# The convolution branch's layer norm between the first units of the seven-product gate, and down sums issued closer together, in a two-layer encoder trunk on one Trainium2 core

## The chip, the core and the metric

The kernel runs on one core of one Trainium2 chip. PE multiplies matrices, DVE and ACT do elementwise work on tiles of 128 partitions, POOL does a little of that and issues DMAs, SP only issues DMAs. Each engine executes its own list of instructions in order and waits for others by semaphores. The metric is device time in microseconds (us), smaller is better; the median of several runs is compared.

## What is computed

Two layers of an encoder over 512 tokens of width 1024, float32. In each, one projection of the normalized input feeds four branches (a convolution branch, neighbourhood, dilated and windowed attention), each of width 256. Every branch is projected to 1024 channels, multiplied by its own sigmoid gate, and the four are summed, projected and added to the input. A ConvFFN follows. Cut to what bears on this change:

```python
def _conformer_conv(a_in, conv_w, conv_b, ln_g, ln_b):
    a, g = jnp.split(a_in, 2, axis=-1)
    u = a * jax.nn.sigmoid(g)
    u = _depthwise_conv(u, conv_w, conv_b)          # width 31
    u = _layernorm(u, ln_g, ln_b)                   # over the 256 channels
    return jax.nn.silu(u)

ys = jnp.stack([y_a, y_b, y_c, y_d], axis=2)
branch = jnp.einsum('bsnc,ncd->bsnd', ys, w_branch[l])
gates = jax.nn.sigmoid(gate_pre.reshape(bsz, seq, N_BRANCH, D_MODEL) + gate_b[l])
mixed = jnp.sum(gates * branch, axis=2)
x = x + mixed @ w_out[l]
x = x + _conv_ffn(_rmsnorm(x, g_ffn[l]), w_up[l], ffn_conv_w[l], ffn_conv_b[l], w_down[l])
```

## The kernel before

**Products and weights.** Activations lie with channels on partitions and the 512 tokens along the free dimension. A float32 product is made of three: the high part of the weights times the high and the low part of the activations, and the low part of the weights times the high part (`prod`, lines 290 to 292). Weights come in units of 128x1024: one load on SP's queue into `w_raw` (two buffers), one ACT instruction for the high half `w_hi` (line 269), one DVE instruction for the low half `w_lo` (line 271), three buffers each. `unit()` asks for a unit one ahead of the one used. A block of 128 output channels is 24 matmuls of 128x128 by 128x512 into one bank. There are eight PSUM banks, four with the tag `mm` and four with `aux`.

**Order.** The program traces the work in one sequence, and a planner turns it into a list for each engine, by priority and by its own estimate of when each instruction is ready. Weight units are put 3000 places ahead. Side work is written as generators. After each half block and each block the main line calls `tick()`: every generator in `side` then runs on to its next `yield`, and what it issues on PE comes after the last matmul so far. `tick()` also adds `self.pace` to a credit (`served`); while that isn't below zero, the next of the down sums is issued and its price, 9, is taken off. `finish(g)` ticks until one generator is done.

**Down sums.** `weight_sums` makes sums of the down projection's weights for a scheme with seven products in place of eight. A layer has 24 transfers between places in DRAM, of 0.75 or 1 MB, copying or accumulating (line 1283). They go on POOL's queue, and each waits for the last matmul at the place where it was traced (`paced`). The credit begins at -40 with a pace of 4.0 where the values are projected; the pace is 2.7 from the end of the windowed attention's projection on.

**The stretch around the change.** In `layer`, after the four branches' projections, `gates(n)` runs for the neighbourhood, dilated and windowed branch (`ORDER[0]`, `[1]`, `[2]`). A gate has eight blocks d. Each block multiplies by the norm (line 860), takes a tanh (line 862) and ticks twice; from d = 2 on, `branch(n, d - 2)` multiplies the branch's output with its own weights (6 matmuls). For the second and third gate line 1005 makes a product of it and the gate on DVE, and line 1006 adds it to `mixed` on POOL. Beside these gates run the attentions and `conv`, the convolution's 60 taps on DVE (line 457), each traced behind a matmul.

When the first half of the third gate and the windowed attention are done, the attention's pool is closed, a pool `outp` is opened, and `gate_forms` is put into `side`: for four pairs of channel blocks, POOL loads the layer's input (line 885, two loads of 256 KB each, paced), ACT multiplies by the gain (line 896), DVE forms four differences and sums (lines 901 to 904), and ACT and DVE split the result (lines 906 and 907). Then the second half of the third gate is traced. `conv`, when its taps are done, goes on to the layer norm as it comes: 8 transposes on PE into two `aux` banks (line 470), statistics on DVE (lines 473 and 474), a Newton iteration for the inverse root (lines 477 and 324 to 329), normalization into `cv` tiles (line 486), 8 transposes back into two `aux` banks (line 495), scale and shift on ACT (line 499), a tanh (line 501) and products and a split (lines 502 to 504) into `Y[0]`. `while self.side: self.tick()` drains all this before the last gate.

**The seven-product gate.** `last_gate` is the convolution branch's gate. `GATE_STEPS` lists 14 units of 24 matmuls of 128x128 by 128x256 (line 935), seven for each half of the channels (`ga`, `gb`): A11 and A12 take the plain input, the others but S4 a form. Each unit ticks twice. Unit A12 uses an `mm` bank for a moment, the others keep four `aux` banks. The raw weights grow in place: after the low half of a unit is made (line 1275), POOL adds the next quarter by an accumulating DMA (line 1256). `gate_done` writes tanh tiles `ths`; after the units 12 and 14 come four branch products each, with `Y[0]`.

Of the kernel before, what the change touches and what calls it, by code (L numbers as in the profile page):

```python
# [14 lines left out]
F32 = mybir.dt.float32  # L15
# [3 lines left out]
ALU = mybir.AluOpType  # L19
# [3 lines left out]
P = 128  # L23
L = 2
D = 1024
S = 512
# [66 lines left out]
ORDER = (1, 2, 3, 0)  # L93
# [137 lines left out]
class Trunk:  # L231
# [214 lines left out]
    def conv(self):  # L446

        nc = self.nc
        v = nc.vector
        accs = []  # L450
        for j in range(2):
            u = self.glu_u[j]
            acc = self.gp.tile([P, 542], F32, name="cv", tag="cv", bufs=4)[:, :S]
            w = lambda t: self.par('a_conv_w', j * 31 + t)
            v.tensor_scalar(acc, u[:, 0:S], w(0), self.par('a_conv_b', j), ALU.mult, ALU.add)
            for t in range(1, 31):
                self.after_mm(v.scalar_tensor_tensor(acc, u[:, t:t + S], w(t), acc, ALU.mult, ALU.add))  # L457
                if t % 5 != 2:
                    yield
            accs.append(acc)  # L460
        yield
        mv = self.norm.tile([P, NB, 2], F32, name="mv", tag="mv", bufs=1)
        st = self.norm.tile([P, NB, 6], F32, name="bst", tag="bst", bufs=1)
        pss = []
        for h in range(2):
            ps = self.aux()
            for b in range(2):
                for j in range(2):
                    tb = 2 * h + b
                    nc.tensor.transpose(out=ps[:, (b * 2 + j) * P:(b * 2 + j + 1) * P],  # L470
                                        in_=accs[j][:, tb * P:(tb + 1) * P], identity=self.ident)
            for b in range(2):
                v.bn_stats(st[:, 2 * h + b, :], ps[:, b * 256:(b + 1) * 256])
                v.bn_aggr(mv[:, 2 * h + b, :], st[:, 2 * h + b, :])
            pss.append(ps)
        ve = self.norm.tile([P, NB], F32, name="ms", tag="ms", bufs=2)
        v.tensor_scalar(ve, mv[:, :, 1], 1.0, EPS, ALU.mult, ALU.add)
        r = self.norm.tile([P, NB], F32, name="rln", tag="rln", bufs=1)
        self.rsqrt(self.norm, ve, [P, NB], r)
        yield  # L480
        uns = []
        for h in range(2):
            un = self.gp.tile([P, 542], F32, name="cv", tag="cv", bufs=4)
            for b in range(2):
                tb = 2 * h + b
                v.tensor_scalar(un[:, b * 256:(b + 1) * 256], pss[h][:, b * 256:(b + 1) * 256], mv[:, tb, 0:1],
                                r[:, tb:tb + 1], ALU.subtract, ALU.mult)
            uns.append(un)
        for _ in range(2):
            yield  # L490
        yh, yl = self.y_tiles()
        for j in range(2):
            ps = self.aux()
            for tb in range(NB):
                nc.tensor.transpose(out=ps[:, tb * P:(tb + 1) * P],
                                    in_=uns[tb // 2][:, (tb % 2) * 256 + j * P:(tb % 2) * 256 + (j + 1) * P],
                                    identity=self.ident)
            z = self.gp.tile([P, 542], F32, name="cv", tag="cv", bufs=4)
            nc.scalar.activation(z[:, :S], ps, AF.Identity, scale=self.par('ln_g', j), bias=self.par('ln_b', j))
            th = self.gp.tile([P, S], F32, name="th", tag="th", bufs=3)  # L500
            nc.scalar.activation(th, z[:, :S], AF.Tanh, scale=0.5)
            v.scalar_tensor_tensor(z[:, :S], th, 1.0, z[:, :S], ALU.add, ALU.mult)
            nc.scalar.activation(yh[:, j, :], z[:, :S], AF.Copy, scale=0.5)
            v.scalar_tensor_tensor(yl[:, j, :], z[:, :S], 0.5, yh[:, j, :].bitcast(F32), ALU.mult, ALU.subtract)
            yield
        self.Y[0] = (yh, yl)
# [433 lines left out]
    def gate_done(self, g, n, ps):  # L940

        nc = self.nc
        v = nc.vector
        if n in ('A11', 'S3', 'S2'):
            tag, bufs = ("th", 3) if n == 'S2' else ("t1", 2) if n == 'A11' else ("xn", 2)
            t = self.svs[g, n] = (self.op if n == 'S3' else self.gp).tile([P, S], F32, name="sv", tag=tag, bufs=bufs)
            with self.first():
                nc.scalar.activation(t, ps, AF.Copy)
        if n == 'S2':
            r, h = 1, 0  # L950
            v.tensor_tensor(t, self.banks[g, 'B'], t, ALU.subtract)
        elif n == 'A12':
            r, h, t = 0, 0, self.svs[g, 'A11']
            v.tensor_tensor(t, t, ps, ALU.add)
        elif n == 'S1':
            r, h, t = 1, 1, self.svs[g, 'S3']
            with self.first():
                v.tensor_tensor(t, t, ps, ALU.subtract)
        elif n == 'S4':
            r, h, t = 0, 1, self.gp.tile([P, S], F32, name="sv", tag="th", bufs=3)  # L960
        else:
            return
        two = lambda t: t.rearrange("p (e q) -> p e q", e=2)
        cols = slice(h * 256, (h + 1) * 256)
        half = self.RB[:, cols].unsqueeze(1).broadcast_to([P, 2, 256])
        v.tensor_tensor(two(t), two(ps if n == 'S4' else t), half, ALU.mult)
        for e in range(2):
            d = 4 * 'ab'.index(g[1]) + 2 * (1 - r) + e
            if h == 0:
                pool, tag, bufs = (self.gp, "cv", 4) if r == 0 else (self.op, "xr", 2) if g == 'ga' else (self.op, "sq", 2)  # L970
                self.ths[d] = pool.tile([P, 542 if r == 0 else S], F32, name="th", tag=tag, bufs=bufs)[:, :S]
            c = ORDER[3] * 8 + d
            nc.scalar.activation(self.ths[d][:, cols], t[:, e * 256:(e + 1) * 256], AF.Tanh, scale=0.5,
                                 bias=self.gbh[:, c:c + 1])
# [12 lines left out]
    def branch(self, n, d, bu, th, q=None):  # L987
        nc = self.nc
        v = nc.vector
        while self.Y[n] is None:  # L990
            self.tick()
        yh, yl = self.Y[n]
        q = d % 4 if q is None else q
        ps = self.mm()
        for k in range(2):
            s = slice((q * 2 + k) * P, (q * 2 + k + 1) * P)
            self.prod(ps, bu[0][:, s], bu[1][:, s], yh[:, k, :], yl[:, k, :], k == 0, k == 1)
        if n == ORDER[0]:
            m = self.gp.tile([P, S], F32, name="mx", tag="mx", bufs=8)
            self.mixed.append(m)  # L1000
            v.scalar_tensor_tensor(m, th, 1.0, ps, ALU.add, ALU.mult)
            return
        m = self.mixed[d]
        t = self.gp.tile([P, S], F32, name="t1", tag="t1", bufs=2)
        v.scalar_tensor_tensor(t, th, 1.0, ps, ALU.add, ALU.mult)
        (v if n == ORDER[3] else nc.gpsimd).tensor_tensor(m, m, t, ALU.add)
        if n == ORDER[3]:
            if d % 2 == 0:
                self.mixed_parts = [self.op.tile([P, 1024], F32R, name=x, tag=f"{x}{d // 2}", bufs=1) for x in ("mh", "ml")]
            mh, ml = (x[:, d % 2 * S:(d % 2 + 1) * S] for x in self.mixed_parts)  # L1010
            nc.scalar.activation(mh, m, AF.Copy, scale=0.5)
            v.scalar_tensor_tensor(ml, m, 0.5, mh.bitcast(F32), ALU.mult, ALU.subtract)
            self.MH[d] = mh, ml
# [550 lines left out]
    def layer(self, l):  # L1564
# [3 lines left out]
        with tc.tile_pool(name="gate", bufs=1, reuse_waits="tile") as self.gp:  # L1568
            with tc.tile_pool(name="attn", bufs=1, reuse_waits="tile") as self.ap:
# [18 lines left out]
                ready = self.beside(self.qk_stats(Q, 4, 4, 0))  # L1588
                self.queue(chain(ready, self.qk_norm(Q, 4, 4, 2), self.attention('dil', Vd, 2)))
                self.glu()  # L1590
                self.side.append(self.conv())
                V = self.new_V()
                Q = self.project_swa(V)
                ready = self.beside(self.qk_stats(Q, 4, 2, 2))
                swa = chain(ready, self.qk_norm(Q, 4, 2, 4), self.attention('swa', V, 3))
                self.queue(swa)
                self.pace = 2.7
                for n in ORDER[:2]:
                    self.gates(n)
                self.gates(ORDER[2], range(4))  # L1600
                self.finish(swa)
            with tc.tile_pool(name="outp", bufs=1, reuse_waits="tile") as self.op:
                self.gate_forms()
                self.gates(ORDER[2], range(4, 8))
                while self.side:
                    self.tick()
                self.last_gate()
                self.pace = 0.0
                self.xnew = self.new_res()
# [82 lines left out]
```

## Time and profile before

| | us |
|---|---|
| median of 3 runs (lowest, highest) | 1567.18 (1567.09, 1567.3) |
| the profiled execution | 1566.39 |
| its span, first to last instruction | 1564.6 |
| PE busy within the span | 1535.1 |
| DVE busy | 1309.2 |
| ACT busy | 942.6 |
| POOL busy | 201.1 |

The mean granted TensorE clock of this execution is 0.992. A line of the time line gives the start in us, the time from the first start to the last end in us, the engine, the line of the kernel, the operation, output and inputs with their shapes, the count and, in brackets, how long the engine stood idle before it and what ended that. Durations of neighbouring matmuls overlap, so the distance of starts says how fast PE goes on.

### The profile page before, as it was taken

How to read it: one execution, taken by the hardware profiler on the slowest of the kernel's cores; microseconds unless marked ns; L12 is line 12 of the kernel's file. 1: busy time of each engine (PE TensorE's matmuls, PEld its weight loads, DVE VectorE, ACT ScalarE, POOL GpSimd, SP SyncE). 2: the span in 40 equal slices, each digit the busy share in tenths (PEclk: the TensorE clock that was granted, in tenths of full speed). 3: DMA queues.
4: the chain of work that ended last, by engine and by line, in shares of the span. 5: the costliest groups of instructions: out<-in, count | busy, mean ns of one | idle time of the engine just before them, and what ended most of it. 6: DMA issues, size and time to landing. Idle time of an engine off the chain costs nothing.

```text
span 1564.6 us, 22903 instructions
## 1 busy us (share of the span) xinstructions
PE 1535.1 (98%) x8274; PEld 1326.2 (85%) x8274; DVE 1309.2 (84%) x2202; ACT 942.6 (60%) x1580; POOL 201.1 (13%) x296
## 2 busy tenths in 40 slices
PE   9999999979999999999999999999799999999999
PEld 8888888859888999888888888888698899998887
DVE  6689988777879998997576899887777899999974
ACT  5678777345456665564457687673454556655643
POOL 0123002322001110000001130023310011100000
PEclk9999999989999999999999999999899999999999
DMA  7788565766565886256558796657666589962564
GB/s 233 226 227 192 158 148 146 188 150 149 185 205 117 183 185 162 97 196 205 183 177 257 202 200 158 141 149 191 151 154 204 187 168 225 196 162 95 185 225 162
DMA packets 117153, 278.58 MB, mean 178 GB/s; under 512 B 27440, under 2 KB 29360, under 8 KB 117040
## 3 DMA queue, kind: packets, MB, share of 16 engines
q1 hardware_dynamic: 87088, 187.98, 37.1%
q0 software_dynamic: 29664, 88.62, 29.1%
q8 instruction: 65, 1.06, 0.3%
q10 hardware_dynamic: 288, 0.52, 0.1%
q14 instruction: 48, 0.39, 0.1%
HBM read 259.25 MB, written 58.72 MB: 203 GB/s over the span
## 4 chain that ended last, share of the span: by engine, by line
PE 87%; DVE 6%; DMA 3%; ACT 3%; issue 1%; POOL 0%; DVEq 0%; ACTq 0%; POOLq 0%
PE mm L291 14%; PE mm L292 14%; PE mm L290 14%; PE aux L1127 9%; PE aux L935 4%; PE aux L1375 3%; PE aux L1374 3%; PE aux L1373 3%; PE mm L519 2%; PE mm L521 2%; PE mm L520 2%; PE mm L1375 2%; PE mm L1374 2%; PE mm L1373 2%; PE aux L812 2%; PE aux L789 2%
## 5 line engine op out<-in xcount | busy, mean ns | idle before, releaser
L269 ACT ACTIVATE w_hi<-w_raw 128x1024 fp32r<-128x1024 f32 (+1 forms) x241 | 251.3, 1043 | 236.0 <-PE mm L291 82.3
L271 DVE TENSOR_TENSOR w_lo<-w_raw,w_hi 128x1024 fp32r<-128x1024 f32 (+1 forms) x241 | 290.9, 1208 | 69.1 <-ACT w_hi L269 67.6
L290 PE MATMUL mm<-xh,w_hi 128*128 128x512 f32 x768 | 300.9, 392 | 0.0
L291 PE MATMUL mm<-xl,w_hi 128*128 128x512 f32 x768 | 300.3, 391 | 0.0
L292 PE MATMUL mm<-xh,w_lo 128*128 128x512 f32 x768 | 299.8, 390 | 0.0
L292 PEld LDWEIGHTS mm<-xh,w_lo 128*128 128x128 f32 x768 | 144.5, 188 | 30.6
L290 PEld LDWEIGHTS mm<-xh,w_hi 128*128 128x128 f32 x768 | 144.7, 188 | 29.1
L291 PEld LDWEIGHTS mm<-xl,w_hi 128*128 128x128 f32 x768 | 144.6, 188 | 28.4
L1127 PE MATMUL aux<-form,w_hi 128*128 128x256 f32 x768 | 140.3, 284 | 0.7 <-ACT sv L1139 0.7
L1127 PEld LDWEIGHTS aux<-form,w_hi 128*128 128x128 f32 x768 | 120.0, 192 | 1.8 <-ACT sv L1139 1.5
L1127 PE MATMUL aux<-form,w_lo 128*128 128x256 f32 x384 | 108.7, 283 | 0.0
L1274 ACT ACTIVATE w_hi<-chain 128x1024 fp32r<-128x1024 f32 x64 | 67.6, 1057 | 57.5 <-DMA chain<-W 15.1
L1275 DVE TENSOR_TENSOR w_lo<-chain,w_hi 128x1024 fp32r<-128x1024 f32 x64 | 77.9, 1219 | 23.1 <-ACT w_hi L1274 23.1
L457 DVE SCALAR_TENSOR_TENSOR cv<-cv,prm 128x512 f32<-128x512 f32 x120 | 94.0, 783 | 0.7
L1168 ACT ACTIVATE cy<-U,prm 128x512 f32<-128x512 f32 x88 | 68.4, 808 | 32.6 <-DVE U L1213 21.0
L519 PE MATMUL mm<-w_hi,xh 128*128 128x512 f32 x192 | 76.4, 398 | 0.4 <-DVE V L647 0.4
L520 PE MATMUL mm<-w_lo,xh 128*128 128x512 f32 x192 | 75.0, 391 | 0.0
L521 PE MATMUL mm<-w_hi,xl 128*128 128x512 f32 x192 | 74.8, 390 | 0.0
L1127 PEld LDWEIGHTS aux<-form,w_lo 128*128 128x128 f32 x384 | 73.7, 192 | 0.0
L1256 POOL DMA_DIRECT2D chain<-W x48 | 42.1, 878 | 240.3 <-DVE w_lo L1275 240.3
L1274 ACT ACTIVATE w_hi<-w_raw 128x1024 fp32r<-128x1024 f32 x48 | 50.6, 1053 | 36.2 <-PE aux L1127 19.8
L776 ACT ACTIVATE e<-e,rl 128x256 f32<-128x256 f32 (+2 forms) x96 | 57.3, 597 | 21.8 <-DVE rl L775 21.4
(376 smaller groups left out, 3865.5 us busy)
## 6 DMA issues: line engine op xcount, KB each, us to landing
w_raw<-W SPq DMA_DIRECT2D x191, 512.0 KB, 4.1
sums<-W POOLq DMA_DIRECT2D x24, 1024.0 KB, 11.5
chain<-W POOLq DMA_DIRECT2D x48, 512.0 KB, 5.4
w_raw<-W SPq DMA_DIRECT2D x66, 256.0 KB, 3.8
w_raw<-sums SPq DMA_DIRECT2D x44, 256.0 KB, 3.6
w_raw<-sums SPq DMA_DIRECT2D x22, 512.0 KB, 4.2
sums<-W POOLq DMA_DIRECT2D x12, 768.0 KB, 8.8
sums<-sums POOLq DMA_DIRECT2D x8, 1024.0 KB, 7.0
```

Of the source, the lines that this page charges most:

```text
L269: w = nc.scalar.activation(hi[:, s], raw[:, s], AF.Copy)
L271: nc.vector.tensor_tensor(lo[:, s], raw[:, s], hi[:, s].bitcast(F32), ALU.subtract)
L290: mm(ps, lhsT=wh, rhs=xh, start=start, stop=False)
L291: mm(ps, lhsT=wh, rhs=xl, start=False, stop=False)
L292: self.last_mm = mm(ps, lhsT=wl, rhs=xh, start=False, stop=stop)
L457: self.after_mm(v.scalar_tensor_tensor(acc, u[:, t:t + S], w(t), acc, ALU.mult, ALU.add))
L519: mm(pss[b], lhsT=self.Xh[k][:, t], rhs=hi[:, s], start=k == 0, stop=False)
L520: mm(pss[b], lhsT=self.Xh[k][:, t], rhs=lo[:, s], start=False, stop=False)
L521: self.last_mm = mm(pss[b], lhsT=self.Xl[k][:, t], rhs=hi[:, s], start=False, stop=k == KT - 1)
L1127: self.last_mm = nc.tensor.matmul(o, lhsT=w[:, s], rhs=x, start=start and not (e or j or i), stop=j == 3 and i == 2, skip_group_check=True)
L1274: nc.scalar.activation(hi, raw, AF.Copy)
L1373: mm(ps, lhsT=x[0], rhs=w[0][:, cols], start=start, stop=False, skip_group_check=again)
```

## The change

It touches the order of the work and some buffers, and no product.

- `conv` waits after its taps until `self.closing` is set, and then makes the layer norm. `closing` is set after the third gate when the forms are done, just ahead of `last_gate`, so that the layer norm's steps are traced at the ticks of the first units of that gate. Only the forms are waited for ahead of it, not all side work.
- The layer norm's four banks are `mm` banks in place of `aux` banks.
- The last gate's tanh tiles of the half with r = 0 lie in `yh` and `yl` buffers in place of `cv` buffers.
- In the third gate, the adds of line 1006 with d of 4 and more, four a layer, go from POOL to DVE.
- The pace of the down sums is 3.6 in place of 2.7 from the first gate on.

```diff
@@ conv
-        yield
+        while not self.closing:
+            yield
...
-            ps = self.aux()
+            ps = self.mm()
...
         yh, yl = self.y_tiles()
         for j in range(2):
-            ps = self.aux()
+            ps = self.mm()
@@ gate_done
-            if h == 0:
-                pool, tag, bufs = (self.gp, "cv", 4) if r == 0 else (self.op, "xr", 2) if g == 'ga' else (self.op, "sq", 2)
-                self.ths[d] = pool.tile([P, 542 if r == 0 else S], F32, name="th", tag=tag, bufs=bufs)[:, :S]
+            if h == 0 and r == 1:
+                self.ths[d] = self.op.tile([P, S], F32, name="th", tag="xr" if g == 'ga' else "sq", bufs=2)
+            elif h == 0 and e == 0:
+                x = self.gp.tile([P, 2, S], F32, name="th", tag="yh" if g == 'ga' else "yl", bufs=2)
+                self.ths[d:d + 2] = x[:, 0], x[:, 1]
@@ branch
-        (v if n == ORDER[3] else nc.gpsimd).tensor_tensor(m, m, t, ALU.add)
+        (v if n == ORDER[3] or n == ORDER[2] and d >= 4 else nc.gpsimd).tensor_tensor(m, m, t, ALU.add)
@@ layer
                 self.glu()
+                self.closing = False
                 self.side.append(self.conv())
...
-                self.pace = 2.7
+                self.pace = 3.6
...
                 self.gate_forms()
+                forms = self.side[-1]
                 self.gates(ORDER[2], range(4, 8))
-                while self.side:
-                    self.tick()
+                self.finish(forms)
+                self.closing = True
                 self.last_gate()
```

## The prediction

> **What bounds the kernel now.** I read the page first, then the waits of PE, then PE's time line where it stops, and last the time lines of ACT, DVE and POOL at those places.
>
> ```profile
> span 1564.6 us, 22903 instructions
> ...
> PE 1535.1 (98%) x8274; PEld 1326.2 (85%) x8274; DVE 1309.2 (84%) x2202; ACT 942.6 (60%) x1580; POOL 201.1 (13%) x296
> ```
>
> PE is busy for 98% of the span, so an edit can only pay where PE stops or where its clock is low. Its idle time is 1564.6 - 1535.1 = 29.5 us. The waits of PE say where (waiter, what ended the wait: us in total, times, longest):
>
> ```profile
> PE aux L495 <- DVE cv L486: 13.0, 2, 6.6
> PE mm L290 <- ACT w_hi L269: 6.4, 2, 4.2
> PE aux L935 <- DVE w_lo L1275: 3.1, 4, 0.9
> ```
>
> Two waits, each once in each layer, make 19.4 us of the 29.5. Both sit at the end of the third gate; line 495 is the second transposition of the layer norm, which the change moves. Here is PE in layer 0:
>
> ```profile
> 328.42 0.80 PE L290 MATMUL mm<-yh,w_hi 128*128 128x512 f32 x1 [4.24 <-ACT w_hi L269]
> 335.64 0.69 PE L495 MATMUL aux<-cst,cv 128*128 128x128 f32 x2 [6.42 <-DVE cv L486]
> ...
> 338.68 0.63 PE L292 MATMUL mm<-yh,w_lo 128*128 128x512 f32 x1
> ...
> 340.39 0.63 PE L290 MATMUL mm<-xh,w_hi 128*128 128x512 f32 x1
> ...
> 345.08 0.39 PE L292 MATMUL mm<-xh,w_lo 128*128 128x512 f32 x1
> ...
> 349.84 0.39 PE L292 MATMUL mm<-yh,w_lo 128*128 128x512 f32 x1
> ```
>
> The reader is to see three losses: PE waits 4.24 us for the high half of a weight unit, then 6.42 us for the normalized tile, and then its clock is halved: from 338.68 to 340.39 matmuls start 0.43 us apart (four steps), from 345.08 to 349.84 they start 0.227 us apart (21 steps). The stretches from the end of the last matmul before the first wait to the first matmul of the seven-product gate give the sum (length; busy time and count of PE, PEld, DVE, ACT, POOL; granted clock, DMA share, GB/s), layer 0 above layer 1:
>
> ```profile
> 324.19:350.07 25.88, 15.23 (x56) 12.03 (x57) 22.21 (x40) 15.47 (x22) 5.62 (x5) 0.74 0.55 117
> 1103.80:1126.33 22.53, 13.78 (x56) 11.03 (x57) 21.13 (x38) 14.09 (x20) 5.65 (x5) 0.77 0.58 130
> ```
>
> Each holds 56 PE instructions, 48 matmuls and 8 transposes. What transposes cost at full clock is seen at the layer norm's first set:
>
> ```profile
> 309.51 1.03 PE L470 MATMUL aux<-cst,cv 128*128 128x128 f32 x8
> 310.30 0.47 PE L290 MATMUL mm<-yh,w_hi 128*128 128x512 f32 x1
> ```
>
> The next matmul starts 0.8 us after the first of the eight. So the work of a stretch is 48 x 0.227 + 0.8 = 11.7 us. **Layer 0 loses 25.9 - 11.7 = 14.2 us, layer 1 22.5 - 11.7 = 10.8 us, together 25.0 us**: 19.4 idle, some 5.6 halved clock. That is the most that can be won here.
>
> The Trainium skill, "TensorE: Matmul & The Clock Gate", section "What's actually happening", has the clock halved after an idle window of about 3.4 us until a busy one of that length. The trace agrees as to the half clock behind the 6.42 us. By that rule a leftover stall under 3.4 us costs only itself, and the sum below would stay as it is.
>
> Why is the weight late? ACT, then POOL, of layer 0:
>
> ```profile
> 324.10 1.37 ACT L896 ACTIVATE xf<-xf,prm 128x512 f32<-128x512 f32 x2 [9.63 <-DMA xf<-xT]
> ...
> 327.33 1.04 ACT L269 ACTIVATE w_hi<-w_raw 128x1024 fp32r<-128x1024 f32 x1
> ```
>
> ```profile
> 308.39 1.16 POOL L1283 DMA_DIRECT2D sums<-W  x1
> 309.97 1.11 POOL L885 DMA_DIRECT2D xf<-xT  x2 [0.42 <-PE mm L292]
> ...
> 321.86 1.01 POOL L1283 DMA_DIRECT2D sums<-W  x1 [2.97 <-PE mm L292]
> 332.51 2.26 POOL L1006 TENSOR_TENSOR mx<-mx,t 128x512 f32<-128x512 f32 x1 [9.64 <-DVE rs_q L328]
> ```
>
> ACT runs in order. It stands 9.63 us before an input tile of the gate's forms; the weight conversion is queued behind it, and PE behind that. The tile was issued at 309.97, right behind a 1 MB down sum on the same queue, and landed at 324.1. The page gives what such loads take otherwise (KB each, median us to landing):
>
> ```profile
> sums<-W POOLq DMA_DIRECT2D x24, 1024.0 KB, 11.5
> ...
> xf<-res POOLq DMA_DIRECT2D x24, 256.0 KB, 3.8
> ```
>
> **The change, part by part.** *Pace 2.7 to 3.6.* Every tick adds the pace to a credit, and each of 24 sums takes 9. The four stages before the first gate make 32 ticks at 4.0: -40 + 128 = 88, so 10 sums are issued and about -2 is left. Fourteen remain; the last needs 2 + 13 x 9 = 119, which is tick 45 at 2.7 and tick 34 at 3.6. The two gates and a half that follow make 16 + 16 + 8 = 40 ticks, and the forms begin at tick 41. So now the last two sums fall among the loads of the forms, as the POOL rows show (308.39 is tick 41, 321.86 tick 45, 3.4 us a tick). Afterwards the last is issued near 308.4 - 7 x 3.4 = 284.6 and has landed near 296, before any load of the forms. The sums stay on POOL's queue and pass eight or so of its adds. SP's queue issues nothing more, but its weight loads share the DMA with denser sums. Whether that hurts is read from two windows, of which the first has the pace of 4.0 and the second that of 2.7, and the third is the seven-product gate:
>
> ```profile
> 59.00:154.00 95.00, 94.58 (x474) 78.85 (x473) 79.81 (x190) 73.14 (x170) 26.41 (x59) 1.00 0.90 233
> 154.00:300.00 146.00, 146.00 (x706) 121.83 (x705) 130.06 (x253) 100.44 (x224) 21.94 (x20) 1.00 0.58 154
> 350.07:401.00 50.93, 49.53 (x373) 47.20 (x372) 39.70 (x46) 28.72 (x41) 10.07 (x10) 1.00 0.65 154
> ```
>
> At 0.90 DMA share PE lost 0.4 us in 95, so I cost the denser sums at nothing; if that cover went, the price is bounded by that rate, 0.4 x 130/95, under 1 us a layer. The gain is the first wait with its part of the cold tail: with a landing of about 4 to 5 us after 309.97 ACT goes on near 315, 9 us earlier, and PE, which ran dry at 324.2, does not.
>
> *Four adds from POOL to DVE.* The rows of line 1006 on both engines:
>
> ```profile
> L1006 POOL TENSOR_TENSOR mx<-mx,t 128x512 f32<-128x512 f32 x32 | 50.5, 1608 | 121.0 <-DVE t L1005 83.6 <-DVE rs_q L328 17.2 <-DVE rl L775 14.3
> ...
> L1006 DVE TENSOR_TENSOR mx<-mx,t 128x512 f32<-128x512 f32 x16 | 10.6, 684 | 0.0
> ```
>
> DVE gets 4 x 0.68 = 2.7 us a layer in a stretch where it is busy for 22.2 of 25.9 us, much of it held up. POOL loses the add at 332.51 that waits 9.64 us, with the last load of the forms queued behind it. What DVE gets back is seen at line 904, whose usual time is 0.41:
>
> ```profile
> 342.11 0.41 DVE L904 TENSOR_TENSOR forms<-xf,forms 128x256 f32<-128x256 f32 x1
> ...
> 354.22 2.94 DVE L904 TENSOR_TENSOR forms<-xf,forms 128x256 f32<-128x256 f32 x1
> ```
>
> ```profile
> 354.01 2.86 POOL L1006 TENSOR_TENSOR mx<-mx,t 128x512 f32<-128x512 f32 x2
> ```
>
> Beside two adds on POOL it took 2.5 us more. So this edit lies between +2.7 and about -2.5 us of DVE time a layer; I take zero, as DVE is not the path here once ACT is free.
>
> The Trainium skill, "SBUF — State Buffer", section "Who interferes with whom", states that a DVE instruction with two SBUF inputs and a GpSimd one that reads SBUF shut each other out. The trace agrees (2.94 against 0.41). By that rule all four adds give back about as much as they cost, and the sum is the same.
>
> *The layer norm, moved to the first units of the seven-product gate.* What moves in a layer (layer 0, counts and busy us):
>
> ```profile
> L486 DVE TENSOR_SCALAR cv<-aux,mv,rln 128x256 f32<-128x256 f32 x4 | 2.0, 529 | 0.0
> ...
> L473 DVE BATCH_NORM_STATS2 bst<-aux 128x6 f32<-128x256 f32 x4 | 1.5, 408 | 0.0
> L499 ACT ACTIVATE cv<-aux,prm 128x512 f32<-128x512 f32 x2 | 1.4, 774 | 2.7 <-PE aux L495 2.7
> ...
> L502 DVE SCALAR_TENSOR_TENSOR cv<-th,cv 128x512 f32<-128x512 f32 x2 | 1.4, 689 | 0.7 <-ACT th L501 0.7
> L504 DVE SCALAR_TENSOR_TENSOR yl<-cv,yh 128x512 fp32r<-128x512 f32 x2 | 1.4, 685 | 0.0
> ...
> L328 DVE TENSOR_TENSOR rs_q<-rs_q,ms 128x4 f32<-128x4 f32 x3 | 0.5, 155 | 0.0
> ```
>
> DVE: 2.0 + 1.5 + 1.4 + 1.4, four aggregations and twelve Newton steps at about 0.16 each (2.5): 8.8 us. ACT: two each of lines 499, 501 and 503, estimated from line 499 at under 4.3 us. PE: 16 transposes, 1.6 us, paid in either place. It issues no DMA. The seven-product gate has DVE busy for 39.7 of 50.9 us and ACT for 28.7; with 8.8 and 4.3 they reach 48.5 and 33.0 at most, less two late forms that move out (two DVE rows of line 904's kind and a 1.2 us split each). So DVE fits, nearly full at the front. The result is needed only at the branch product after the twelfth unit, 12 x 2.9 us on (a unit is 24 matmuls; 350.07 to 401.00 holds 14 of them and eight branch blocks).
>
> What is late next: the second transposition now stands between units on PE and waits for line 486, behind DVE's weight halves, forms and sums; all later matmuls queue behind it. The trace does not show this wait at its new place. Its ends: below nothing (the gate's 3.1 us of waits for DVE could shrink with the POOL adds gone, 1.5 a layer) and 6.6 us a layer, the wait as it is today. I take 3 us a layer, because the chain of 6 us on DVE lies beside two to three units of PE work but shares DVE with their halves.
>
> The buffers cost nothing: the last gate's tanh tiles go into buffers of earlier branches' outputs, whose readers are done by the gate's start; the transposes use the four banks of the blocks, free but for one short user.
>
> Sum: 25.0 won - 2 x 3 = 19.0 us. The profiled execution took 1566.39 us around its span of 1564.6, so 1547.4 for it; the median of the runs is 1567.18, 0.8 above. **Forecast 1548 us**, own range 1543 to 1553.
>
> **The rivals.** *The wait moves along.* The transposes wait at their new place as long as now, 6.5 us, with a cold tail of about 3 us: 2 x 9.5 = 19 given back instead of 6, 1561 us. For it: DVE is the busier engine at the new place; against: the planner has 12 units to place them in, and DVE's standstill behind the forms' loads, which made 6.4 today, is gone. Half of that is 1555.
>
> *The load stays late.* If the forms' tiles still hold ACT, 4.24 and 2.19 us and some 2 us of cold clock each stay: about 10 us, 1558. For it: the loads are still queued behind PE's pace; against: the median landing of 3.8 us. That the change does not do what it says, sums still among the loads, is this case with the other wait unchanged too: 1567.
>
> *Slower.* The layer norm's 8.8 us on DVE get ahead of the first units' low halves. Each raw tile grows by DMA only after its low half is made (A11, S3, S2, S4 one after another), so a delay at the first is carried on to all. Per layer 8.8 for the delay, 6.6 for the transposes and 3.5 of halved clock make 18.9: 1567.2 - 25 + 37.8 = 1580. It decides from 12.5 us of new stall a layer on. Against: the gate's waits for low halves are 0.8 us each now (3.1 in four), with DVE busy for 78% of the gate.
>
> **How the numbers follow.** Forecast 0.57; better than 1543, with the gate's own waits gone too (1541 to 1543), 0.07; part given back or the load still late, 1553 to 1562, 0.22; no change 0.07; slower 0.07. A measurement of this kernel can tell about 0.2%, 3 us. Faster is 0.57 + 0.07 + 0.22 less 0.01 for its edge: 0.85; within 0.2%, 0.08; slower 0.07. The range 1541 to 1560 leaves out the last two cases and the end of the third.
>
> **What would show it.** In the new profile: no sums after the first load of the forms; ACT's waits for those loads under 3 us; no wait of PE for line 269's unit; PE clock at 1.0 through both stretches; line 495's transposes among the gate's matmuls with a wait of about 3 us; line 1006 with 24 adds on POOL and 24 on DVE. I am wrong if PE waits over 5 us at line 495 or at the first units for low halves, or if PE stops in the first two gates for weights.

## The result and the profile after

| | before | after |
|---|---|---|
| median, us | 1567.24 (4 runs, 1567.09 to 1567.31) | 1544.51 (4 runs, 1543.59 to 1545.78) |
| ratio to before | | 0.9856, 95% interval 0.9839 to 0.9873 |
| the profiled execution, us | 1566.39 | 1543.59 |
| its span, us | 1564.6 | 1541.8 |
| mean granted TensorE clock | 0.992 | 1.0 |

The forecast was 1548 us in a range from 1541 to 1560. The number came out; the account of where it comes from did not, as the experiments show. One execution of a later kernel (the second transposition two ticks later, with pace and adds) took 2550 us at a granted clock of 0.556 and is in no ratio.

The page of the changed kernel, its span and the row of busy time:

```profile
span 1541.8 us, 22905 instructions
...
PE 1528.9 (99%) x8274; PEld 1322.0 (86%) x8274; DVE 1308.0 (85%) x2210; ACT 942.8 (61%) x1580; POOL 187.7 (12%) x288
```

The idle time of PE fell from 29.5 to 12.9 us, and its busy time by 6.2 us, since no matmul runs at half clock any more. The waits of PE:

```profile
PE aux L936 <- DVE w_lo L1278: 3.3, 4, 1.0
PE mm L496 <- DVE cv L487: 2.0, 2, 1.0
PE aux L1130 <- ACT sv L1142: 1.4, 2, 1.1
```

Line 496 is line 495 of before, line 936 line 935. The wait of 13.0 us is 2.0 us now, and the one for line 269 is gone. PE's time line of layer 0, from the branch product that stood 4.24 us for its weights to the first matmul of the seven-product gate:

```profile
322.30 0.39 PE L290 MATMUL mm<-yh,w_hi 128*128 128x512 f32 x1
...
333.18 0.28 PE L936 MATMUL aux<-xh,w_hi 128*128 128x256 f32 x1
```

These are the 48 matmuls of the stretch that took 25.9 us before, in 10.9 us, which is 48 x 0.227: nothing is lost there. The sums and the loads of the forms on POOL, and ACT's second pair of loads:

```profile
283.39 0.95 POOL L1286 DMA_DIRECT2D sums<-W  x1 [2.57 <-PE mm L292]
...
306.46 0.63 POOL L886 DMA_DIRECT2D xf<-X  x1 [0.21 <-issue]
307.08 0.57 POOL L886 DMA_DIRECT2D xf<-xT  x1
309.23 1.07 POOL L886 DMA_DIRECT2D xf<-xT  x2 [1.58 <-PE mm L292]
```

```profile
312.14 1.39 ACT L897 ACTIVATE xf<-xf,prm 128x512 f32<-128x512 f32 x2 [0.52 <-DMA xf<-xT]
```

The last sum goes out at 283.39, 23 us ahead of the first load, and ACT waits 0.52 us where it waited 9.63.

### The profile page after: what moved, and what is told of

The parts are those of the page before. It is cut to its first block, busy times and chain, and to the rows that moved or that the text cites. A ratio compares the mean times of both kernels' runs of the same rounds, so it can differ in the third digit from the quotient of the medians.

```text
span 1541.8 us, 22905 instructions
## 1 busy us (share of the span) xinstructions
PE 1528.9 (99%) x8274; PEld 1322.0 (86%) x8274; DVE 1308.0 (85%) x2210; ACT 942.8 (61%) x1580; POOL 187.7 (12%) x288
## 3 DMA queue, kind: packets, MB, share of 16 engines
q8 instruction: 65, 1.06, 0.3%
## 4 chain that ended last, share of the span: by engine, by line
PE 85%; DVE 8%; ACT 3%; issue 2%; DMA 2%; POOL 0%; ACTq 0%; DVEq 0%; POOLq 0%
PE mm L291 14%; PE mm L290 14%; PE mm L292 14%; PE aux L1130 11%; PE aux L936 3%; PE aux L1376 3%; PE aux L1378 3%; PE aux L1377 3%; PE mm L520 2%; PE mm L521 2%; PE mm L522 2%; PE mm L1376 2%; PE mm L1378 2%; PE mm L1377 2%; PE mm L1130 2%
```

## The experiments

Three theories were held against each other. S: two separate causes, the sums for the first wait and the layer norm's place for the second; this is how the prediction shared out the gain. C: one common cause, the late load, which stops ACT and through it DVE, where the normalization is queued behind the forms. N: the layer norm's place makes both.

The change has three parts, and all their combinations were run. "Pace" is 3.6 for 2.7, "adds" the four adds on DVE, "norm" the layer norm with its banks and the tanh tiles' buffers.

| parts in | us | before, measured with it | ratio, 95% interval |
|---|---|---|---|
| pace | 1545.22 | 1567.27 | 0.9869 (0.9852 to 0.9885) |
| norm | 1568.68 | 1567.27 | 1.0012 (1.0003 to 1.0021) |
| adds | 1565.83 | 1567.27 | 0.9990 (0.9981 to 0.9999) |
| pace, adds | 1544.43 | 1567.27 | 0.9860 (0.9845 to 0.9875) |
| pace, norm | 1552.36 | 1566.47 | 0.9912 (0.9897 to 0.9927) |
| norm, adds | 1561.99 | 1566.47 | 0.9972 (0.9960 to 0.9984) |
| all three | 1544.51 | 1567.24 | 0.9856 (0.9839 to 0.9873) |

### Pace alone

```diff
-                self.pace = 2.7
+                self.pace = 3.6
```

> Only the pace of the sums is raised (3.6), the layer norm and the adds stay. Theory S (separate causes: the sums hold the forms' load, the layer norm's own place makes the second wait): the first wait (4.24 and 2.19 us) and some 3 us of cold clock go, the 13.0 us at the transposes stay: about 1558 us. Theory C (common cause: the late load also stops DVE, and the normalization stands behind the forms there): both waits shrink to 1 or 2 us, 1544 to 1549. Theory N (the layer norm's place alone makes both): 1565 to 1567.

Measured: 1545.22 us, 22.05 below before. One number did what the whole change does; this is theory C. The waits of PE:

```profile
PE aux L495 <- DVE cv L486: 3.5, 2, 1.7
PE aux L935 <- DVE w_lo L1275: 3.3, 4, 0.9
```

The layer norm stands where it stood, and its wait fell from 13.0 to 3.5 us. DVE's time line shows why. First the kernel before, in layer 0:

```profile
316.57 0.16 DVE L325 TENSOR_SCALAR rln<-rs_i 128x4 int32<-128x4 int32 x1
325.50 0.43 DVE L901 TENSOR_TENSOR forms<-xf 128x256 f32<-128x256 f32 x1 [8.78 <-ACT xf L896]
325.84 0.15 DVE L327 SCALAR_TENSOR_TENSOR rs_q<-rln 128x4 f32<-128x4 f32 x1
...
335.05 1.44 DVE L486 TENSOR_SCALAR cv<-aux,mv,rln 128x256 f32<-128x256 f32 x3
```

Then the same places with the higher pace:

```profile
315.78 0.16 DVE L325 TENSOR_SCALAR rln<-rs_i 128x4 int32<-128x4 int32 x1
315.85 0.41 DVE L901 TENSOR_TENSOR forms<-xf 128x256 f32<-128x256 f32 x1
316.19 0.15 DVE L327 SCALAR_TENSOR_TENSOR rs_q<-rln 128x4 f32<-128x4 f32 x1
...
325.40 1.44 DVE L486 TENSOR_SCALAR cv<-aux,mv,rln 128x256 f32<-128x256 f32 x3
```

The reader is to look at line 901 between two steps of the Newton iteration. DVE runs its list in order; a form whose input ACT hadn't scaled yet held up the next Newton step, and so the normalization, by 9 us. The wait names line 486 as the culprit, and its cause is a DMA two engines away. The pace has not changed the order of this list: from 309 us to the end of line 486 both time lines hold the same instructions in the same order.

### Norm alone, adds alone, pace and adds

The first leaves the pace and the adds of the change out and has the rest, whose core is

```diff
-        yield
+        while not self.closing:
+            yield
```

The second is this line alone, the third this line and the pace:

```diff
-        (v if n == ORDER[3] else nc.gpsimd).tensor_tensor(m, m, t, ALU.add)
+        (v if n == ORDER[3] or n == ORDER[2] and d >= 4 else nc.gpsimd).tensor_tensor(m, m, t, ALU.add)
```

> Only the layer norm is moved; the pace is 2.7 and the adds stay on POOL. Theory S: the 13.0 us at the transposes go, the wait for line 269's unit stays (6.4 us and a cold tail of some 3): about 1552 to 1554. Theory C: the late load still holds ACT and DVE, so that at least the 6.4 us stay and forms or low halves are late in the next gate: 1553 to 1560. Theory N: 1544 to 1547.

> Only the four adds a layer go to DVE. Theory S and N: within 1 us of 1567. Theory C the same, less up to 2 us, as the last load of the forms no longer waits behind an add on POOL. A rival (the adds on POOL are the cause of the late Newton steps, through DVE standing still beside them): 1560 or less.

> The pace and the adds, the layer norm as before. Theory S: 1558. Theory C: 1543 to 1548, no more to win by moving the layer norm. Theory N: 1565 to 1567.

Measured: norm alone 1568.68, 1.4 us above before and above every theory's range, C's too; adds alone 1565.83, 1.4 us below before, which is as C had it; pace and adds 1544.43, within C's range. The waits of PE with the norm alone:

```profile
PE mm L290 <- ACT w_hi L269: 9.4, 2, 4.7
PE aux L936 <- DVE w_lo L1278: 6.6, 8, 2.8
PE mm L471 <- DVE t L861: 4.3, 2, 2.7
```

The 13.0 us at the second transposition are gone, but the late load still stops PE for 9.4 us, at the first transposition DVE is behind by 4.3, and in the gate the low halves are late by 3.5 us more than before. So a wait can be removed without its time being won, as long as its cause is there. Not all of the loss is the late load's: one wait of 2.81 us in the gate stands in the next run as well, where the load is in time.

### Pace and norm; norm and adds

The first is the change without the line of the adds, the second the change with a pace of 2.7.

> The whole change but for the adds, which stay on POOL. If the adds matter little: 1544 to 1546. If four adds on POOL hold DVE's forms and low halves up in the first units of the gate: 1548 to 1552.

> The whole change but for the pace (2.7). Theory S: the wait for line 269's unit with its cold tail is back, 1552 to 1554. Theory C: as S or up to 1560. Theory N: 1544 to 1546.

Measured: 1552.36 and 1561.99, the first 0.4 us above the higher of its two ranges, the second 2 us above C's. Without the adds on DVE the moved layer norm costs 7 us against the pace alone (1545.22; the ratios to before are 0.9912 and 0.9869); with them it costs nothing. At a pace of 2.7 the adds help it too, from 1568.68 to 1561.99. What the trace shows for pace and norm, PE, DVE, POOL and ACT in layer 0:

```profile
347.62 0.39 PE L936 MATMUL aux<-form,w_lo 128*128 128x256 f32 x1 [2.81 <-DVE w_lo L1278]
```

```profile
342.09 0.17 DVE L478 TENSOR_SCALAR ms<-mv 128x4 f32<-128x4 f32 x1
...
346.35 1.22 DVE L1278 TENSOR_TENSOR w_lo<-chain,w_hi 128x1024 fp32r<-128x1024 f32 x1
```

```profile
336.75 4.78 POOL L1009 TENSOR_TENSOR mx<-mx,t 128x512 f32<-128x512 f32 x3 [5.97 <-DVE t L1008]
341.48 0.90 POOL L1259 DMA_DIRECT2D chain<-W  x1
```

```profile
351.23 1.45 ACT L500 ACTIVATE cv<-mm,prm 128x512 f32<-128x512 f32 x2 [5.20 <-PE mm L496]
352.57 1.05 ACT L1277 ACTIVATE w_hi<-chain 128x1024 fp32r<-128x1024 f32 x1
```

And the same steps in the changed kernel, DVE, POOL and ACT:

```profile
342.57 1.22 DVE L1278 TENSOR_TENSOR w_lo<-chain,w_hi 128x1024 fp32r<-128x1024 f32 x1
343.70 0.16 DVE L478 TENSOR_SCALAR ms<-mv 128x4 f32<-128x4 f32 x1
```

```profile
337.77 0.89 POOL L1259 DMA_DIRECT2D chain<-W  x1 [8.75 <-DVE w_lo L1278]
```

```profile
346.66 1.06 ACT L1277 ACTIVATE w_hi<-chain 128x1024 fp32r<-128x1024 f32 x1 [2.35 <-PE aux L936]
```

PE's waits in the gate are 8.1 us in this run, 3.3 in the changed kernel, and 5.6 of the 8.1 are this wait of 2.81 us, once in each layer. It is for the low half of the first unit with a form. ACT has that unit's high half ready at 342.67 (it starts at 341.61 and takes 1.06), but DVE makes the low half only at 346.35: most of the layer norm's Newton iteration, which begins with line 478, stands ahead of it in DVE's list. In the changed kernel the iteration stands behind it, and the low half comes 1.6 us after the high one. The two other runs with the norm moved agree: with the adds on POOL (norm alone) the iteration is ahead, and PE waits 2.81 and 1.36 us there; with them on DVE (norm and adds) it is behind.

Two more things are late in this run, for a later unit. Three adds stand on POOL ahead of the load that makes the second raw tile grow, and it goes out 3.7 us later; 2.9 of these are DVE's, as the low half that it waits for ends at 340.38 in place of 337.48. On ACT's list the weight conversion of that unit stands behind the layer norm's scaling, which waits 5.20 us for PE's transposes, and is 5.9 us later. PE's wait for that unit is only 0.44 us (at 355.21). The orders are the planner's, and they were not tried one by one. So the wait of 2.81 us is read from the trace; why moving four adds changes DVE's order, and what each order costs alone, is open.

### The loads of the forms on SP's queue

```diff
-                    self.paced(nc.gpsimd.dma_start(x[:, e * S:(e + 1) * S], self.xres[2 * j + e]))
+                    self.paced(nc.sync.dma_start(x[:, e * S:(e + 1) * S], self.xres[2 * j + e]))
```

> The kernel before with one edit: the loads of the forms go out on SP's queue, still paced, in place of POOL's. If it is the place behind a 1 MB sum on POOL's queue that makes the load late, it lands in 4 to 6 us, the first wait goes, and the time is as with the higher pace alone (1558 by theory S, 1544 to 1549 by theory C). If it is the shared bandwidth of the 16 DMA engines, the load still lands after 10 us or more, and the time stays at 1565 to 1568. A loss is possible too: the pacing now holds the weight loads behind it on SP.

Measured: 1561.77 us, ratio 0.9973 (0.9962 to 0.9984), between the two. The sums stay where they were, among the loads, and PE's waits are:

```profile
PE aux L495 <- DVE cv L486: 13.4, 2, 6.7
PE mm L290 <- ACT w_hi L269: 2.0, 2, 1.4
```

The time to landing of these loads is 3.8, 7.2 and 11.8 us (least, median, most), against 3.1, 5.4 and 14.2 before and 2.9, 3.0 and 3.7 with the higher pace. So taking the loads off the sums' queue did not bring them back to 3 us; in the median they were later. SP's queue is no empty one, though: it carries the weight units, and one of them, issued at 304.52, is ahead of the forms' first load and lands, by the trace, at 312.22. From then on the first four loads land about 2 us apart (ACT takes them at 315.71, 317.95, 320.12 and 321.40), while a sum issued on POOL at 306.81 is in flight until 321.04. That fits bandwidth shared with the sum, but the run doesn't part it from what SP's own queue adds. The first wait shrank to 2.0 us, the second did not, since DVE still met unscaled forms.

### A still higher pace

```diff
-                self.pace = 3.6
+                self.pace = 5.0
```

> The changed kernel with a pace of 5.0. If denser sums are hidden in the first two gates: 1543 to 1546 as with 3.6. If they take bandwidth that the weight units or the attention's tiles need: over 1548, with waits of PE for line 269 or 520 in the first gates.

Measured, in the changed kernel: 1544.89 us, ratio 0.9865 (0.9850 to 0.9879). The last sum of layer 0 goes out at 238.29, 45 us earlier than with 3.6. No wait of PE for line 269 appears, the one at line 520 is 0.3 us, and one in the attention is 1.4 us where it was 0.3. Denser sums are hidden in the first two gates.

### No sums while the forms are loaded

```diff
                 self.gate_forms()
+                self.pace, self.served = 0.0, self.served - 100.0
                 self.gates(ORDER[2], range(4, 8))
                 while self.side:
                     self.tick()
+                self.pace, self.served = 2.7, self.served + 100.0
```

> The kernel before, pace 2.7 as it was, but no sum is issued while the forms are loaded: the last two of each layer come in the seven-product gate. Theory C (only the sums among the forms' loads matter): both waits of PE go as with the higher pace, 1545 us, more by what two late sums cost beside the gate's accumulating loads (0 to 5 us): 1545 to 1550. If it is the denser spacing in the first two gates that helps in some other way: 1562 or more.

Measured: 1560.62 us, ratio 0.9959 (0.9944 to 0.9974). The waits of PE:

```profile
PE aux L935 <- ACT w_hi L1274: 7.9, 2, 5.4
PE aux L495 <- DVE cv L486: 4.5, 2, 2.8
```

The spacing in the gates is that of before, and still the wait for line 269 is gone and the one at the transposes is 4.5 us: it is the two sums among the loads that matter, not the spacing. The total missed its range of 1545 to 1550, and the two sums now stand among the accumulating loads of the seven-product gate. Layer 0, POOL and then ACT:

```profile
341.69 1.06 POOL L1283 DMA_DIRECT2D sums<-W  x1
343.46 0.92 POOL L1256 DMA_DIRECT2D chain<-W  x1 [0.71 <-DVE w_lo L1275]
...
347.45 0.97 POOL L1283 DMA_DIRECT2D sums<-W  x1 [0.50 <-PE aux L935]
```

```profile
358.59 1.06 ACT L1274 ACTIVATE w_hi<-chain 128x1024 fp32r<-128x1024 f32 x1 [5.72 <-DMA chain<-W]
```

The load that ACT waits for is the one of 343.46, right behind the first sum; it takes 15.0 us to land, where the median of the loads into these tiles is 5.6 in this run. So a 1 MB sum makes the same kind of wait at the next place where a load is urgent.

What such a wait costs beside itself is seen in the windows (columns as in the prediction), here from 348 to 372 us, and below them in the run with pace and norm, first around its wait of 2.81 us in layer 0, then behind the same wait in layer 1, which ends at 1117.37:

```profile
348.00:360.00 12.00, 6.64 (x54) 6.44 (x54) 6.68 (x9) 5.52 (x10) 2.20 (x3) 0.89 1.09 217
360.00:372.00 12.00, 10.79 (x73) 10.28 (x73) 4.58 (x4) 4.48 (x7) 2.63 (x3) 0.82 0.97 182
```

```profile
344.00:350.00 6.00, 3.15 (x25) 2.74 (x25) 5.83 (x15) 1.54 (x2) 0.87 (x1) 1.00 0.68 169
1118.00:1124.00 6.00, 6.00 (x40) 5.98 (x40) 2.77 (x5) 1.68 (x3) 1.35 (x2) 0.75 0.79 134
```

After 5.4 us of standstill the granted clock is 0.89 and 0.82. After 2.81 us it is 1.00 in layer 0 and 0.75 in layer 1, where matmuls start 0.21 us apart in place of 0.12 for some 3 us. The Trainium skill, "TensorE: Matmul & The Clock Gate", section "What's actually happening", puts the step at an idle window of about 3.4 us. The 5.4 us agree with it; the 2.81 us of layer 1 do not, so in this run a wait shorter than that window cost clock in one layer of two.

### The forms four ticks later

```diff
+            for _ in range(4):
+                yield
             load(0)
             yield
```

> The kernel before, but the forms begin four ticks later, so that DVE's list has the Newton steps and the normalization ahead of the forms; sums and pace as before. Theory C: the 13.0 us at the transposes go or shrink under 3 us although the layer norm stays where it was, while loads of the forms can still be late and stop PE at a later unit. Theory S (the layer norm's own length at this place makes the wait): the 13.0 us stay. The total isn't the reading here, as late forms can cost at the gate: 1550 to 1572.

Measured: 1569.76 us, ratio 1.0014 (1.0005 to 1.0023). This separates S and C best. The layer norm is at its place of before, the sums and the pace too; but DVE's list has the normalization ahead of the forms, and it runs at 318.63:

```profile
318.63 1.90 DVE L486 TENSOR_SCALAR cv<-aux,mv,rln 128x256 f32<-128x256 f32 x4
```

PE has no wait at the second transposition at all. The load is still late (ACT waits 9.61 us for it at 340.48), and PE pays for it in the gate instead:

```profile
PE mm L937 <- DVE t L860: 8.9, 2, 6.7
PE aux L937 <- DVE w_lo L1277: 7.7, 6, 2.4
```

### The second transposition two ticks later

```diff
-        for _ in range(2):
+        for _ in range(4):
             yield
```

> The kernel before with the pace of 3.6 and the four adds on DVE, the layer norm at its old place, with two more ticks between normalization and second transposition. The 3.5 us that PE waited for at the transposes in this variant without the ticks should go: 1541 us. If the planner places them by readiness and not by the tick: 1544, no change.

> The changed kernel with two more ticks between normalization and second transposition. The 2.0 us that PE waits for at the transposes should go: 1542.5 us; if the output of the layer norm then holds ACT's weight halves up: 1546 or more.

Measured: 1542.79 us, ratio 0.9840 (0.9827 to 0.9854), for pace and adds with the layer norm at its old place. PE has no wait at line 495 in it. For the changed kernel with the later transposition 1543.77 us, ratio 0.9847 (0.9833 to 0.9860); the wait of 2.0 us at line 496, which was expected to go, stayed. The intervals overlap each other and that of the changed kernel, so neither is shown to be faster than it. That the layer norm can stay where it was at no loss is shown.

## Why the prediction was right, and where it was not

**What was there to win: right.** 25.0 us in the two stretches; the profiled executions differ by 1566.39 - 1543.59 = 22.8.

**The sums' place: right.** Forecast near 284.6, measured 283.39; ACT went on at 312.1, forecast near 315.

**Which edit wins it: wrong.** The step that failed is "The gain is the first wait with its part of the cold tail", for the pace. The rest, the 13.0 us at the transposes, was given to the moving of the layer norm. The pace alone won 22.05 us, the norm alone lost 1.4, and with the pace already there it won nothing. The rows for it were in hand: the prediction named "DVE's standstill behind the forms' loads, which made 6.4 today", but as an argument against a rival, and did not carry it back into the share of the pace. The total was spared because all parts came at once; that it came out is no evidence for the split.

**The new wait of the transposes: mis-sized.** The term was 3 us a layer; it measured 1.0. With it at 1.0 the sum is 25.0 - 2.0 = 23.0, 0.2 from the profiled difference.

**The adds at zero: wrong for the kernel they are in.** Alone they gave 1.4 us, about nothing, as costed. In company of the moved layer norm they are worth 7.9 us (1552.36 against 1544.51, ratios 0.9912 and 0.9856). The reason given was that "DVE is not the path here once ACT is free". With the norm moved and the adds left on POOL it was: the 2.81 us that PE waits in each layer end on a low half that DVE makes behind the Newton iteration.

**The rivals.** "The wait moves along" came as 2.0 us, not 13. "The load stays late" didn't happen with the pace, and is what the runs without it show (9.4 and 9.9 us with the norm moved). "Slower" happened in a small way where the norm moved without the pace, and its mechanism, layer norm work on DVE ahead of the first units' low halves, is PE's wait on that low half in both runs where the norm moved and the adds did not.

**The clock behind a short wait: not borne out.** The prediction worked with "a leftover stall under 3.4 us costs only itself". A wait of 2.81 us was followed by half clock in layer 1 of the run with pace and norm. It changed nothing in the sum, as no wait of the changed kernel at these places is over 1.0 us.

**The signs named beforehand.** Clock 1.0, no wait for line 269, 24 adds on each engine (the page has 288 POOL and 2210 DVE instructions, eight fewer and eight more), no sums after the first load: all as said. The wait of the second transposition, named at about 3 us, was 1.0.

## What to carry to other kernels

Before sharing a gain between edits, follow each wait back past the engine that is named to the first instruction that waited for something outside; two waits of one engine can have one cause. A small load that an in-order engine needs soon should not share its moment with large transfers; moving these earlier, where there is slack, was worth 22 us here, moving them later gave 6.6 and brought a wait back elsewhere, and moving the small loads to another busy queue gave 4.7. And run the parts of a change alone: of the three here one did all, and one of the others was needed only to make the third harmless.

## What was not expected of the hardware

A load of 256 KB of the forms took 3.0 us in the median and at most 3.7 with no sum beside it (pace alone; 3.1 and 4.6 in the changed kernel), at most 14.2 us behind a 1 MB sum on its queue, and still at most 11.8, 7.2 in the median, from SP's queue beside the same sums and behind weight units. That another queue would help so little was not expected. Nor was it that the same wait of 2.81 us would leave the clock at 1.00 in one layer and halve it in the other.
